# Block products for six of sixteen k-tile pairs in the second product of both MLPs of a two-layer decoder

## The chip, the cores and the metric

The kernel runs on one core of a Trainium2 chip. The metric is the device time of one execution in microseconds. The engines named below are PE (TensorE, matmuls; its weight loads are shown apart as PEld), DVE (VectorE), ACT (ScalarE), POOL (GpSimd) and SP (SyncE, which issues the DMAs here).

## What is computed

The reference is a decoder of two layers on 256 tokens with 1024 features, all in float32. Each layer is a mixer (attention on the tokens, differential in layer A and with one shared K/V in layer B, and attention to a fixed memory of 256 rows), and then an MLP of 1024 to 4096 to 1024:

```python
def _sq_relu_mlp(h, w_up, w_down):
    u = jax.nn.relu(h @ w_up)
    return (u * u) @ w_down

# in each layer, after the mixer has been added to x
x = x + _sq_relu_mlp(_rmsnorm(x, a_norm_mlp[i]), a_w_up[i], a_w_down[i])
```

The change concerns the product `(u * u) @ w_down`: 256 x 4096 times 4096 x 1024, once in layer A and once in layer B.

## The kernel before, in words

**Precision.** Each float32 operand is split into a high part, rounded to the fast matmul type (fp32r), and the rest (low). A product is made of three passes: high by high, low by high, high by low. For weights, ACT makes the high part of a chunk of 128 x 1024 (`wh`, a cast, L330), and DVE subtracts it from the chunk to get the low part (`wl`, L332); both stand in `chunk`. There are 192 chunks in the order of use, four buffers `w` for what the DMAs bring, and six each for `wh` and `wl`.

**Layouts.** The residual `xT` is held turned, features on the partitions (8 tiles of 128 x 256 tokens). `mlp_up` computes u turned as well, 32 tiles (k) of 128 hidden units by 256 tokens, each with its high and its low part (the tiles B, `us`). Its scaling, squaring and splitting on ACT and DVE are L779 to L793.

**Second product of layer A** (`mlp`, in `wide`, L805 and L809). The weights are the stationary operand. For each of 8 output tiles m there are 4 chunks of 8 k-tiles; a k-tile costs one matmul over 512 columns (high weights by both parts of u side by side) and one over 256 (low weights by high u). The result is already turned and is added to `xT` by `add_x`, tile by tile, so norms and statistics of layer B (`done`) start while later tiles are computed.

**Second product of layer B** (`mlp_last`, L861). The output is in natural layout, tokens on the partitions: the parts of u are stationary (128 tokens at a time, index hf), the weights move with 512 columns (index c). Four accumulators (hf, c) in PSUM, the banks `t`, take 32 k-tiles of three matmuls each. The last `HELD` = 6 k-tiles are kept back and done cell by cell, so that the final norm of one cell runs beside the products of the next. The residual has been turned to natural layout before by 16 transposes (L845).

**Order of the work.** The kernel is written as steps with an engine, an estimated time and keys for what they read and write. `Plan.order` then places them by list scheduling: among ready steps of an engine the lowest priority number goes first, and the number is the place in the program less a shift from the table `EARLY`, one for each kind of step and layer (`w` is the splitting of weights, `nat` the products of a mixer, `stat` the statistics, and so on). Buffers of a class are handed out in order. The engines then run their instructions in that fixed order and wait on semaphores. The stationary loads (PEld) run beside the matmuls.

Of the kernel before, what the change touches and what calls it, by code (L numbers as in the profile page):

```python
# [24 lines left out]
HELD = 6  # L25
CW = 1024
# [5 lines left out]
EARLY.update(wA=14, wB=40, memA=-47, memB=133, natA=84, natB=18, statA=-67, statB=98, ropeA=-143, ropeB=-86,  # L32
             scoreA=-56, scoreB=-10, ptA=23, ptB=73, pvB=-40, finA=160, finB=-72, evacA=46, evacB=53, prepA=151,
             prepB=46, normA=96, normB=44)
# [185 lines left out]
def t_mm(n, passes=1):  # L220
    return passes * (n / 2.4 + 13.5)
# [3 lines left out]
def tile_hybrid(ctx: ExitStack, tc: tile.TileContext, xa, xb, memt, xnat, mnat, w0, wall, consts, fgain, out):  # L225
    nc = tc.nc
# [20 lines left out]
    def bank(cls):  # L247
        return buf(cls, [128, 512], F32, psum)
# [4 lines left out]

    def fixed(shape, nm, dt=F32):
        return const.tile(shape, dt, name=name(nm))
# [18 lines left out]
    vb = fixed([128, 2, 12, 64], "vb")  # L274

# [356 lines left out]
    def plain_T(p, rs, causal):  # L632
# [4 lines left out]
        if par is None:  # L637
            pp = [Buf("ppa", lambda slot: ppx[:, slot]) for _ in range(2)]
        else:
            pp = [part(par, "ppb", 512) for _ in range(2)]  # L640
# [127 lines left out]
    def mlp_up(st):  # L768
# [4 lines left out]
        for b in range(16):  # L773
# [16 lines left out]
            P.add(("act", t_act(512), lambda u=u: nc.scalar.activation(u.t, u.t, AF.Square)), [u], [u])  # L790
            P.add(("act", t_act(512), lambda u=u, t=us[b // 2], k0=k0: nc.scalar.copy(t.t[:, k0:k0 + 2, 0], u.t)),
# [6 lines left out]
    def ukeys(us, k):  # L798
        return [(us[k // 4], k // 2), (us[k // 4], k // 2, 1)]
# [16 lines left out]

    def mlp(st, done):
        us = mlp_up(st)
        for m in range(8):
            ps = bank("acc")  # L820
            for c in range(4):
                wh, wl = chunk()
                wide(ps, wh, wl, lambda k, c=c: us[2 * c + k // 4].t[:, k % 4], lambda k, c=c: ukeys(us, 8 * c + k),
                     c == 0, c == 3)
            add_x(m, ps, 0)
            add_x(m, ps, S)
            done(m)
        st_["pieces"] = 2

    def mlp_last(st):  # L830
# [19 lines left out]
        us = mlp_up(st)  # L850
        pss = {cell: bank("t") for cell in cells}
        ch = []

        def mm(k, hf, c, c0=0, c1=512, ps=None, k0=0):
            wh, wl = ch[k]
            ps = ps or pss[hf, c]

            def emit():
                uh, ul = [us[k // 4].t[:, k % 4, i, hf * 128:(hf + 1) * 128] for i in range(2)]
                for i, (a, b) in enumerate(((uh, wh), (ul, wh), (uh, wl))):  # L860
                    nc.tensor.matmul(ps.t[:, c0:c1], a, b.t[:, c * 512 + c0:c * 512 + c1],  # L861
                                     start=(k == k0 and i == 0), stop=(k == 31 and i == 2), skip_group_check=True)
            P.add(("pe", t_mm(c1 - c0, 3), emit), ukeys(us, k) + [(wh, c), (wl, c)], [ps])
        held = 32 - HELD
        for k in range(32):
            ch.append(chunk())
            if k < held:
                for hf, c in cells:
                    mm(k, hf, c)
# [3 lines left out]
        for hf in range(2):  # L873
            ss, part_, r = fixed([128, 4], "ss"), fixed([128, 1], "part"), fixed([128, 1], "rstd")
            for c in range(2):
# [5 lines left out]
                for i in range(2):  # L881
                    if last:
                        for k in range(held, 32):
                            mm(k, hf, c, 256 * i, 256 * i + 256, tail if i else None, held if i else 0)
                        ps = tail if i else ps
# [271 lines left out]
def _layout(inp):  # L1157
# [18 lines left out]
    def down(w):  # L1176
        return w.reshape(4, 8, 128, 8, 128).transpose(3, 0, 2, 1, 4).reshape(32, 128, CW)
# [49 lines left out]
```

## Time and profile before

| | us |
|---|---|
| three runs | 605.34, 606.75 (median), 984.32 |
| the profiled execution | 606.42 |
| its span, first to last instruction | 604.6 |
| PE busy in the span | 592.3 (98%) |
| DVE busy | 438.6 (73%) |
| ACT busy | 377.2 (62%) |

The span is what the trace shows; the profiled execution's own time is 1.8 us longer. Shares of busy time are means over stages with different limits. A matmul's recorded duration holds its way through the array, and the next one begins before it ends, so what a row of matmuls costs is read from start to start. In the same way a DVE instruction may begin a little before the recorded end of the one ahead of it.

In time order the span holds: the mixer of layer A to about 127 us, the first product of its MLP to 216 us, the second to 305 us, the mixer of layer B to about 420 us, the first product of its MLP to 510 us, the second to 596 us, and the final norm and output.

### The profile page before, as it was taken

How to read it: one execution, taken by the hardware profiler on the slowest of the kernel's cores; microseconds unless marked ns; L12 is line 12 of the kernel's file. 1: busy time of each engine (PE TensorE's matmuls, PEld its weight loads, DVE VectorE, ACT ScalarE, POOL GpSimd, SP SyncE). 2: the span in 40 equal slices, each digit the busy share in tenths (PEclk: the TensorE clock that was granted, in tenths of full speed). 3: DMA queues.
4: the chain of work that ended last, by engine and by line, in shares of the span. 5: the costliest groups of instructions: out<-in, count | busy, mean ns of one | idle time of the engine just before them, and what ended most of it. 6: DMA issues, size and time to landing. Idle time of an engine off the chain costs nothing.

```text
span 604.6 us, 9476 instructions
## 1 busy us (share of the span) xinstructions
PE 592.3 (98%) x3430; PEld 505.1 (84%) x3430; DVE 438.6 (73%) x800; ACT 377.2 (62%) x771; POOL 55.6 (9%) x67
## 2 busy tenths in 40 slices
PE   8999999999999999999999999999999999999995
PEld 6778878988888888888888887889888888888884
DVE  6689997689887865656777788876888787544435
ACT  6878787576766654444665776776686666443422
POOL 0031020140000000101001123001300000000002
PEclk9989999999999999999999999999999999999998
DMA  8964733436655555555566435344565555555501
GB/s 317 335 206 149 261 108 107 156 129 206 217 201 181 201 178 197 185 186 194 180 208 237 145 105 171 109 140 147 185 226 178 197 184 194 189 185 198 191 20 69
DMA packets 29999, 108.39 MB, mean 179 GB/s; under 512 B 3328, under 2 KB 3328, under 8 KB 29696
## 3 DMA queue, kind: packets, MB, share of 16 engines
q1 hardware_dynamic: 29664, 107.26, 52.9%
q8 instruction: 27, 0.44, 0.3%
q10 hardware_dynamic: 288, 0.52, 0.2%
q14 instruction: 20, 0.16, 0.1%
HBM read 106.72 MB, written 1.05 MB: 178 GB/s over the span
## 4 chain that ended last, share of the span: by engine, by line
PE 93%; DMA 3%; DVE 2%; ACT 1%; issue 0%; SPq 0%; ACTq 0%
PE acc L805 29%; PE acc L493 19%; PE acc L809 15%; PE t L861 14%; PE acc L759 7%; DMA w<-wall 3%; PE t L580 2%; PE t L618 2%; PE t L675 1%; PE t L551 1%; DVE wl L332 1%; DVE xT L745 0%; ACT wh L330 0%; PE acc L861 0%; PE t L845 0%
## 5 line engine op out<-in xcount | busy, mean ns | idle before, releaser
L332 DVE TENSOR_TENSOR wl<-w,wh 128x512 fp32r<-128x512 f32 (+1 forms) x256 | 245.4, 979 | 116.7 <-ACT wh L330 114.3
L330 ACT CAST wh<-w 128x512 fp32r<-128x512 f32 (+1 forms) x256 | 208.8, 840 | 177.1 <-PE acc L805 90.6
L805 PE MATMUL acc<-xn,wh 128*128 128x512 f32 x512 | 131.3, 396 | 0.5 <-DVE xn L348 0.5
L805 PEld LDWEIGHTS acc<-xn,wh 128*128 128x128 f32 x512 | 91.1, 188 | 18.5 <-DVE xn L348 1.8
L493 PE MATMUL acc<-wh,xn 128*128 128x512 f32 x256 | 86.1, 401 | 0.9 <-ACT xn L346 0.9
L861 PE MATMUL t<-wh,B 128*128 128x512 f32 (+1 forms) x256 | 77.2, 384 | 0.0
L809 PEld LDWEIGHTS acc<-xn,wl 128*128 128x128 f32 x512 | 68.1, 188 | 5.6
L809 PE MATMUL acc<-xn,wl 128*128 128x256 f32 x512 | 69.1, 277 | 0.0
L805 PE MATMUL acc<-B,wh 128*128 128x512 f32 x256 | 64.1, 392 | 0.0
L493 PEld LDWEIGHTS acc<-wh,xn 128*128 128x128 f32 x256 | 48.0, 188 | 12.9 <-issue 1.5
L861 PEld LDWEIGHTS t<-wh,B 128*128 128x128 f32 x256 | 47.7, 188 | 9.5
L805 PEld LDWEIGHTS acc<-B,wh 128*128 128x128 f32 x256 | 46.0, 189 | 8.2
L493 PE MATMUL acc<-wl,xn 128*128 128x512 f32 x128 | 50.4, 394 | 0.1
L759 PE MATMUL acc<-B,wh 128*128 128x256 f32 x256 | 50.5, 289 | 0.0
L861 PE MATMUL t<-wl,B 128*128 128x512 f32 (+1 forms) x128 | 49.2, 384 | 0.0
L759 PEld LDWEIGHTS acc<-B,wh 128*128 128x128 f32 x256 | 41.0, 191 | 1.0 <-issue 0.8
L446 POOL TENSOR_TENSOR sqa<-sqa,sq 128x256 f32<-128x256 f32 x21 | 20.7, 988 | 226.5 <-ACT sq L445 225.9
L809 PEld LDWEIGHTS acc<-B,wl 128*128 128x128 f32 x256 | 34.9, 190 | 2.5
L759 PE MATMUL acc<-B,wl 128*128 128x256 f32 x128 | 36.1, 282 | 0.0
L527 POOL TENSOR_TENSOR ropet<-ropes,consts 128x256 f32<-128x256 f32 (+1 forms) x28 | 25.0, 912 | 120.4 <-ACT ropes L516 98.4
L809 PE MATMUL acc<-B,wl 128*128 128x256 f32 x256 | 35.7, 282 | 0.0
L599 ACT ACTIVATE B<-t,nm 128x128 f32<-128x128 f32 (+1 forms) x64 | 27.0, 441 | 7.6 <-DVE nm L595 5.7
(179 smaller groups left out, 727.1 us busy)
## 6 DMA issues: line engine op xcount, KB each, us to landing
w<-wall SPq DMA_DIRECT2D x191, 512.0 KB, 3.3
w<-memt SPq DMA_DIRECT2D x4, 512.0 KB, 4.8
B<-xnat SPq DMA_DIRECT2D x1, 1024.0 KB, 7.8
B<-mnat SPq DMA_DIRECT2D x1, 1024.0 KB, 8.3
xT<-xa SPq DMA_DIRECT2D x1, 540.0 KB, 3.6
w<-w SPq DMA_DIRECT2D x2, 256.0 KB, 3.6
xT<-xb SPq DMA_DIRECT2D x1, 512.0 KB, 6.3
consts<-consts SPq DMA_DIRECT2D x1, 256.5 KB, 4.4
```

Source lines behind the costliest of these rows:

```text
L330: P.add(("act", t_act(n), lambda sl=sl: nc.scalar.copy(h.t[:, sl], w.t[:, sl])), [(w, x) for x in q], [(h, x) for x in q])
L332: P.add(("dve", t_dve(n), lambda sl=sl: nc.vector.tensor_sub(l.t[:, sl], w.t[:, sl], h.t[:, sl].bitcast(F32))), [(w, x) for x in q] + [(h, ...
L446: P.add(("pool", t_pool(S), lambda: nc.gpsimd.tensor_tensor(self.acc.t, self.acc.t, sq.t, op=OP.add)), [sq, self.acc], [self.acc])
L493: nc.tensor.matmul(pss[hf].t[:, c0:c1], a(k)[:, ts], b.t[:, o + c0:o + c1], start=(k == 0 and i == 0), stop=(k == KT - 1 and i == 2))
L527: nc.gpsimd.tensor_tensor(t.t[:, 0:nh, e:e + 32], zs.t[:, 0:nh, 32 - e:64 - e], b(sin[:, e:e + 32]), op=OP.mult)
L580: nc.tensor.matmul(sp[hd].t[:, c], qk[a].t[r, qb * 128:(qb + 1) * 128], qk[b].t[r, S:S + c.stop - c.start], start=(qb == 0 and i == 0 and ...
L599: nc.scalar.activation(p[hd].t[:, c], sp[hd].t[:, c], AF.Exp, bias=nm[hd][:, qb:qb + 1], accum_out=ss[:, hd, qb:qb + 1])
L618: nc.tensor.transpose(ps.t[:, i * 128:(i + 1) * 128], p.t[:, j * 128:(j + 1) * 128], ident)
L759: nc.tensor.matmul(o, a.t[:, ws], x(k), start=(n == 0 and m % 2 == 0 and i == 0), stop=(n == KT - 1 and i == 2), skip_group_check=True)
L805: nc.tensor.matmul(ps.t, wh.t[:, k * 128:(k + 1) * 128], x(k).rearrange("p a s -> p (a s)"), start=start and k == 0, stop=stop and k == 7, ...
L809: nc.tensor.matmul(ps.t[:, 0:S], wl.t[:, k * 128:(k + 1) * 128], x(k)[:, 0], start=False, stop=stop and k == 7, skip_group_check=True)
L861: nc.tensor.matmul(ps.t[:, c0:c1], a, b.t[:, c * 512 + c0:c * 512 + c1], start=(k == k0 and i == 0), stop=(k == 31 and i == 2), skip_group ...
```

## The change

In both MLPs the second product treats the pairs of k-tiles 1, 3, 5, 7, 9 and 11 of 16 (`FAST`) as a product of two 2 x 2 matrices of blocks: 2 halves of the tokens by 2 k-tiles, times 2 k-tiles by 2 halves of the output columns. Instead of 8 block products it makes 7, of sums and differences of the blocks (Strassen's scheme, in Winograd's form). A block product is three matmuls of 512 columns, as before.

The four sums of blocks of u that this takes are made in the first product by four subtractions and additions of 128 x 128 on DVE (`block_sums`, in `mlp_up`); they are kept in buffers that are idle there (`ppx`, `vb`, `mv`), and are split into high and low in the second product, into tiles of `xn`. Four sums of weight blocks are made by DVE from the two loaded chunks (`diff`, four of 128 x 512, into the new buffer `wsum`), and then three chunks and a half are split for such a pair where two were. Four more accumulators, the banks `acc` (`more`), take the partial products, and `gather` adds them into the outputs after pair 11.

The second product of layer A takes the natural layout of layer B's (`natural_down`). Its last 8 k-tiles are done for output columns 0 to 511 first and then for 512 to 1023, with the weights laid out for that in `down`. Each half is added to the gathered part, turned back by transposes (8 for a half), and added to `xT`. The table `EARLY` has other numbers for all kinds of steps.

```diff
+FAST = (1, 3, 5, 7, 9, 11)
...
-EARLY.update(wA=14, wB=40, memA=-47, memB=133, natA=84, natB=18, statA=-67, statB=98, ropeA=-143, ropeB=-86,
+EARLY.update(wA=40, wB=-21, memA=20, memB=31, natA=25, natB=64, statA=-44, statB=-119, ropeA=-90, ropeB=9, scoreA=-92,
...
+            if b in sums:
+                dst, keys = sums[b]
+                def blocks(u=u, dst=dst):
+                    a = [u.t[:, k, hf * 128:hf * 128 + 128] for hf in range(2) for k in range(2)]
+                    s = [dst()[:, i * 128:i * 128 + 128] for i in range(4)]
+                    nc.vector.tensor_add(s[0], a[2], a[3])
+                    nc.vector.tensor_sub(s[1], s[0], a[0])
+                    nc.vector.tensor_sub(s[2], a[0], a[2])
+                    nc.vector.tensor_sub(s[3], a[1], s[1])
...
+        def fast_pair(n, j):
...
+            split(0, wb(0, 0), [wk[0]], 512)
+            diff(0, wb(0, 1), wb(0, 0), wk[:2])
+            split(1, lambda: w[1].t, wk[2:])
+            diff(1, wb(1, 1), lambda: t(0), [wk[3]] + rk(0))
+            split(2, lambda: t(0, 2), rk(0) + rk(1))
+            diff(2, wb(1, 1), wb(0, 1), [wk[1], wk[3]])
+            diff(3, wb(1, 0), lambda: t(1), [wk[2]] + rk(1))
+            split(3, lambda: t(2, 4), rk(2) + rk(3))
...
+            for ps, a, ak, x, c, last in (
+                    (more[0], u_(2 * j, 0), k0, 0, 0, end), (pss[0, 0], u_(2 * j + 1, 0), k1, 1, 0, False),
+                    (pss[0, 1], s_(3), ks, 1, 1, False), (more[1], s_(0), ks, 2, 0, end),
+                    (more[2], s_(1), ks, 2, 1, end), (more[3], s_(2), ks, 3, 0, end),
+                    (pss[1, 0], u_(2 * j + 1, 1), k1, 3, 1, False)):
+                product(ps, a, wcol(x, c), 0, 512, last, ak + [h[x], l[x]])
...
     def mlp(st, done):
-        us = mlp_up(st)
-        for m in range(8):
-            ps = bank("acc")
-            for c in range(4):
-                wh, wl = chunk()
-                wide(ps, wh, wl, lambda k, c=c: us[2 * c + k // 4].t[:, k % 4], lambda k, c=c: ukeys(us, 8 * c + k),
-                     c == 0, c == 3)
-            add_x(m, ps, 0)
-            add_x(m, ps, S)
-            done(m)
+        us = mlp_up(st, block_sums())
...
+        for c in range(2):
+            for k in range(part, 32):
...
+            for hf in range(2):
+                y, ps = ys[hf, c], pss[hf, c]
+                P.add(("dve", t_dve(512), lambda y=y, ps=ps: nc.vector.tensor_add(y.t, y.t, ps.t)), [y, ps], [y])
...
+                            nc.tensor.transpose(ps.t[:, i * S + hf * 128:i * S + hf * 128 + 128],
+                                                ys[hf, c].t[:, o:o + 128], ident)
```

Three places show how the order of instructions moves. On DVE, within the second product of layer A, the row before is that of two output tiles; `xT` and `xn` are the residual and the next layer's input:

```order
L332 TENSOR_TENSOR wl_2670<-w_2586,wh_2661 128x1024
L348 SCALAR_TENSOR_TENSOR xn_67<-xT_66,xn_67 128x256
L332 TENSOR_TENSOR wl_2695<-w_2608,wh_2687 128x1024
L332 TENSOR_TENSOR wl_2717<-w_2630,wh_2709 128x1024
L745 TENSOR_TENSOR xT_66<-xT_66,acc_2642 128x256
L332 TENSOR_TENSOR wl_2742<-w_2659,wh_2731 128x1024
```

Now one pair done as before and one fast pair fill this row (L338 is the old subtraction, L902 the sums of weight blocks, L895 the subtractions of the fast pair):

```order
L902 TENSOR_TENSOR wsum_78<-w_2916 128x512
L338 TENSOR_TENSOR wl_2947<-w_2875,wh_2941 128x1024
L902 TENSOR_TENSOR wsum_78<-w_2928,wsum_78 128x512
L902 TENSOR_TENSOR wsum_78<-w_2928,w_2916 128x512
L902 TENSOR_TENSOR wsum_78<-w_2928,wsum_78 128x512
L338 TENSOR_TENSOR wl_2973<-w_2904,wh_2961 128x1024
L895 TENSOR_TENSOR wl_2980<-w_2916,wh_2968 128x512
L895 TENSOR_TENSOR wl_2987<-w_2928,wh_2978 128x1024
L895 TENSOR_TENSOR wl_2999<-wsum_78,wh_2992 128x1024
L895 TENSOR_TENSOR wl_3011<-wsum_78,wh_3004 128x1024
```

The same ten rows stand there once for each of the later pairs of pairs; the earlier ones have a subtraction of 128 x 512 more, for the sums of u (L921).

On PE, at the end of the second product of layer A (L871, into the `t` banks), rows of the memory's keys and values for layer B (L499, into `acc`) now stand between the last products and the transposes that turn the second half (L990; `ql` holds the two cells of that half):

```order
L871 MATMUL t_2596<-wh_3128,B_518_2557 128x512 x2
L871 MATMUL t_2596<-wl_3135,B_518_2557 128x512
L499 MATMUL acc_3284<-wh_3250,wh_3148 128x512
L499 MATMUL acc_3284<-wl_3268,wh_3148 128x512
L499 MATMUL acc_3284<-wh_3250,wl_3154 128x512
L499 MATMUL acc_3296<-wh_3250,wh_3148 128x512
L499 MATMUL acc_3296<-wl_3268,wh_3148 128x512
L499 MATMUL acc_3296<-wh_3250,wl_3154 128x512
L499 MATMUL acc_3284<-wh_3261,wh_3148 128x512
L499 MATMUL acc_3284<-wl_3280,wh_3148 128x512
L499 MATMUL acc_3284<-wh_3261,wl_3154 128x512
L990 MATMUL t_3325<-ident_122,ql_3071 128x128
```

Before, the products of layer A ended and all 48 of the memory block followed, with no transpose among them.

On SP, the loads at the start of the kernel (`xnat` and `mnat` are the tokens and the memory in natural layout, for their statistics, `memt` the memory turned, `wall` the chunks of weights) stood in this order:

```order
L307 DMA consts_68<-consts 128x513
L307 DMA w_282<-wall 128x1024
L307 DMA w_298<-wall 128x1024
L307 DMA w_311<-wall 128x1024
L307 DMA B_133_325<-xnat 128x2048
L307 DMA w_354<-wall 128x1024
L307 DMA w_367<-memt 128x1024
L307 DMA w_376<-memt 128x1024
L307 DMA w_388<-wall 128x1024
L307 DMA B_147_401<-mnat 128x2048
```

With the new table they stand in this one:

```order
L313 DMA consts_68<-consts 128x513
L313 DMA B_126_283<-xnat 128x2048
L313 DMA w_310<-wall 128x1024
L313 DMA w_321<-wall 128x1024
L313 DMA w_333<-wall 128x1024
L313 DMA w_345<-wall 128x1024
L313 DMA B_138_353<-mnat 128x2048
L313 DMA w_382<-memt 128x1024
L313 DMA w_406<-memt 128x1024
L313 DMA w_417<-wall 128x1024
```

The tokens in natural layout have moved ahead of three chunks of weights, and the memory in natural layout ahead of the turned memory and of the first chunk that the memory block uses.

## Rows read from the trace of the kernel before

**Rows 1.** The page's head and busy time of two engines over the span.

```profile
span 604.6 us, 9476 instructions
...
PE 592.3 (98%) x3430; PEld 505.1 (84%) x3430; DVE 438.6 (73%) x800; ACT 377.2 (62%) x771; POOL 55.6 (9%) x67
```

**Rows 2.** PE in time around layer A's second product: start, duration, instructions.

```profile
215.66 1.99 PE L805 MATMUL acc<-B,wh 128*128 128x512 f32 x8
217.49 1.12 PE L809 MATMUL acc<-B,wl 128*128 128x256 f32 x8
...
304.08 1.12 PE L809 MATMUL acc<-B,wl 128*128 128x256 f32 x8
305.03 0.40 PE L493 MATMUL acc<-wh,wh 128*128 128x512 f32 x1
```

**Rows 3.** The chain that ended last, layer B's second product: start, length.

```profile
510.47 85.13 PE t L861 x384
```

**Rows 4.** PE in time there: start, duration; three matmuls from 511.01 to 511.69.

```profile
511.01 0.61 PE L861 MATMUL t<-wh,B 128*128 128x512 f32 x2
511.46 0.39 PE L861 MATMUL t<-wl,B 128*128 128x512 f32 x1
511.69 0.61 PE L861 MATMUL t<-wh,B 128*128 128x512 f32 x2
```

**Rows 5.** PE in time, eight of the 16 transposes ahead of layer B's MLP.

```profile
419.25 1.03 PE L845 MATMUL t<-ident,xT 128*128 128x128 f32 x8
420.04 0.71 PE L805 MATMUL acc<-xn,wh 128*128 128x512 f32 x2
```

**Rows 6.** Stretches: us; busy (count) of PE, PEld, DVE, ACT, POOL; clock; DMA.

```profile
0.00:20.00 20.00, 17.88 (x94) 14.31 (x95) 13.70 (x32) 12.89 (x25) 0.44 (x5) 1.00 0.88 327
...
127.00:216.00 89.00, 88.50 (x515) 76.99 (x514) 75.09 (x114) 61.63 (x104) 5.48 (x6) 1.00 0.58 190
216.00:306.00 90.00, 90.00 (x517) 79.15 (x516) 55.94 (x74) 44.41 (x66) 5.97 (x6) 1.00 0.57 190
```

**Rows 7.** DVE in time, first product of layer A: start, duration.

```profile
149.30 1.23 DVE L332 TENSOR_TENSOR wl<-w,wh 128x1024 fp32r<-128x1024 f32 x1
150.44 0.41 DVE L781 TENSOR_TENSOR u<-u,acc 128x256 f32<-128x256 f32 x1
150.77 1.22 DVE L332 TENSOR_TENSOR wl<-w,wh 128x1024 fp32r<-128x1024 f32 x1
151.91 0.68 DVE L793 TENSOR_TENSOR B<-u,B 128x512 fp32r<-128x512 f32 x1
152.51 0.68 DVE L787 SCALAR_TENSOR_TENSOR u<-u,rb 128x512 f32<-128x512 f32 x1
153.11 0.41 DVE L781 TENSOR_TENSOR u<-u,acc 128x256 f32<-128x256 f32 x1
```

**Rows 8.** Groups of the span: busy, mean ns; idle before, and its releaser.

```profile
L332 DVE TENSOR_TENSOR wl<-w,wh 128x1024 fp32r<-128x1024 f32 x128 | 157.5, 1230 | 97.5 <-ACT wh L330 97.5
L330 ACT CAST wh<-w 128x1024 fp32r<-128x1024 f32 x128 | 134.7, 1052 | 148.1 <-PE acc L805 89.7 <-PE t L861 40.6 <-PE acc L759 16.6
```

**Rows 9.** PE in time near the start: first uses of the memory block's weights.

```profile
28.04 0.40 PE L493 MATMUL acc<-wh,xn 128*128 128x512 f32 x1
29.01 0.50 PE L493 MATMUL acc<-wh,wh 128*128 128x512 f32 x1 [0.57 <-ACT ropes L516]
31.74 0.79 PE L493 MATMUL acc<-wl,wh 128*128 128x512 f32 x1 [2.23 <-DVE wl L332]
...
34.03 0.63 PE L493 MATMUL acc<-wh,wh 128*128 128x512 f32 x1
34.46 0.48 PE L493 MATMUL acc<-wl,wh 128*128 128x512 f32 x1
```

**Rows 10.** The chain that ended last, near the start: two loads of weights.

```profile
9.54 5.62 DMA w<-wall
...
20.33 6.72 DMA w<-wall
```

More of the change, by code (lines that the diff above doesn't have):

```diff
@@ L31 @@
 EARLY = {k + l: 0 for k in KINDS for l in "AB"}
[L32 to L34 removed]
+EARLY.update(wA=40, wB=-21, memA=20, memB=31, natA=25, natB=64, statA=-44, statB=-119, ropeA=-90, ropeB=9, scoreA=-92,
+             scoreB=-56, ptA=128, ptB=-59, pvA=-41, pvB=145, finA=153, finB=85, evacA=38, evacB=167, prepA=148,
+             prepB=38, normA=120, normB=40)
 LOOK = 100
@@ L252, in part, with ppx_buf @@
         return Buf(cls, lambda slot: parent.t[:, slot, 0:width], parent)
+    def ppx_buf():
+        return Buf("ppa", lambda slot: ppx[:, slot])
     def fixed(shape, nm, dt=F32):
@@ L274, in tile_hybrid @@
     vb = fixed([128, 2, 12, 64], "vb")
+    wsum = fixed([128, 2048], "wsum")
     ones_b = fixed([128, 128], "ones_b", BF)
@@ L637, in plain_T @@
         if par is None:
-            pp = [Buf("ppa", lambda slot: ppx[:, slot]) for _ in range(2)]
+            pp = [ppx_buf() for _ in range(2)]
         else:
@@ L766, in out_proj, with mlp_up @@
                 done(m)
-    def mlp_up(st):
+    def mlp_up(st, sums=()):
         st.rstd()
@@ L790, in mlp_up @@
             P.add(("act", t_act(512), lambda u=u: nc.scalar.activation(u.t, u.t, AF.Square)), [u], [u])
+            if b in sums:
[7 more added lines that the diff above has]
+                    nc.vector.tensor_sub(s[3], a[1], s[1])
+                P.add(("dve", 4 * t_dve(128) + 100, blocks), [u], keys, port=True)
             P.add(("act", t_act(512), lambda u=u, t=us[b // 2], k0=k0: nc.scalar.copy(t.t[:, k0:k0 + 2, 0], u.t)),
@@ L815, in wide, with block_sums @@
                   [x for j in range(k, k + 4) for x in keys(j)] + [(wl, k // 4)], [ps])
-    def mlp(st, done):
-        us = mlp_up(st)
-        for m in range(8):
-            ps = bank("acc")
-            for c in range(4):
-                wh, wl = chunk()
-                wide(ps, wh, wl, lambda k, c=c: us[2 * c + k // 4].t[:, k % 4], lambda k, c=c: ukeys(us, 8 * c + k),
-                     c == 0, c == 3)
-            add_x(m, ps, 0)
-            add_x(m, ps, S)
-            done(m)
+    def block_sums():
+        sums = {}
+        for i, j in enumerate(FAST):
+            if i < 2:
+                b = ppx_buf()
+                dst, keys = (lambda b=b: b.t), [b]
+            elif i < 5:
+                dst = lambda i=i: vb.rearrange("p a b e -> p (a b e)")[:, (i - 2) * 512:(i - 1) * 512]
+                keys = [("vb", n, hf) for n in range(2) for hf in range(2)]
+            else:
+                dst, keys = (lambda: mv.rearrange("p a b e -> p (a b e)")), [("mv", 0), ("mv", 1)]
+            sums[j] = dst, keys + [("s", j)]
+        st_["sums"] = sums
+        return sums
@@ L849, in mlp_last, with gather, add, to @@
             xs[hf, c] = x
-        us = mlp_up(st)
+        us = mlp_up(st, block_sums())
         pss = {cell: bank("t") for cell in cells}
[L852 to L863, printed above, removed]
-        held = 32 - HELD
[L865 to L869, printed above, removed]
+        def gather(more):
+            v = buf("u", [128, 2, S])
+            vt = lambda: v.t.rearrange("p a s -> p (a s)")
+            def add(dst, a, b, r, w, port=False):
+                P.add(("dve", t_dve(512), lambda: nc.vector.tensor_add(dst(), a(), b())), r, w, port=port)
+            def to(cell, src, key, port=False):
+                x = xs[cell]
+                add(lambda: x.t, lambda: x.t, src, [(x, 0), (x, 1), key], [(x, 0), (x, 1)], port)
+            r1, r5, r6, r7 = more
+            P.add(("act", t_act(512, True), lambda: nc.scalar.copy(vt(), r1.t)), [r1], [v])
+            to((0, 0), lambda: r1.t, r1)
+            add(vt, vt, lambda: r6.t, [v, r6], [v])
+            to((0, 1), vt, v, True)
+            to((0, 1), lambda: r5.t, r5)
+            to((1, 1), lambda: r5.t, r5)
+            add(vt, vt, lambda: r7.t, [v, r7], [v])
+            to((1, 0), vt, v, True)
+            to((1, 1), vt, v, True)
+        held = 32 - HELD
+        mm = natural_down(us, pss, 32, held, gather, wsum, lambda a: [("wsum", a)], 4)[0]
         x, ps, tail = xs[1, 1], pss[1, 1], bank("acc")
@@ L883, in mlp_last @@
                         for k in range(held, 32):
-                            mm(k, hf, c, 256 * i, 256 * i + 256, tail if i else None, held if i else 0)
+                            mm(k, hf, c, 256 * i, 256 * i + 256, tail if i else None)
                         ps = tail if i else ps
@@ L1176, in down @@
     def down(w):
-        return w.reshape(4, 8, 128, 8, 128).transpose(3, 0, 2, 1, 4).reshape(32, 128, CW)
+        w = w.reshape(32, 128, CW)
+        return np.concatenate([w[:24], w[24:].reshape(4, 2, 128, 2, 512).transpose(3, 0, 2, 1, 4).reshape(8, 128, CW)])
     def mix(q, k, v, qm, mem, second):
```

96 lines of the change are left out of this document (added).

## The prediction

> **What bounds the kernel now.** I read the page first: the span is 604.6 us, PE is busy for 98% of it and DVE for 73% [rows 1]. Busy PE may still be slow PE, so next came PE in time, from start to start. In layer A's second product eight wide and eight narrow matmuls follow one another without a gap from 215.66 to 305.03 us, and the mixer's products begin at once behind them [rows 2]: 89.4 us for 32 chunks, 2.79 us each. In layer B's second product three matmuls of 512 columns start every 0.68 us, 0.2267 us each [rows 4], and the chain that ended last runs through 384 of them in one piece of 85.1 us [rows 3]. So in both stages nothing but the number of columns sets the time. The only idle time of PE that a change of order can touch lies near the start: 0.57 and 2.23 us at 28 to 32 us [rows 9], where a load of weights ended the wait [rows 10]. The forecast is therefore a count of matmuls, if DVE, which gets most of the new work, keeps up.
>
> **Layer A's products.** In natural layout 32 k-tiles cost 4 cells by 3 matmuls each, 384. A fast pair makes 7 x 3 = 21 where two k-tiles made 24, so six save 18, and 366 are left. At 0.2267 us that is 83.0 us, against 89.4: minus 6.4 us. Of this 4.1 are the block products; 2.3 are the layout, whose 384 would take 87.1 us, because the wide form's 2.79 us for a chunk is more than 12 x 0.2267 = 2.72. The new transposes, 16 in all, are like those ahead of layer B's MLP, where eight take 0.79 us from start to start [rows 5]: plus 1.6 us. Three changes of matmul kind around them I put at 0.1 us each, an estimate from the 0.1 us of a transpose: plus 0.3. Layer A: minus 4.5 us.
>
> The Trainium skill, "TensorE: Matmul & The Clock Gate", Part 4, gives about 275 ns for a transpose in a kernel. By that the 16 cost 4.4 us and layer A gains 1.7. The trace does not agree: the starts are 0.1 us apart [rows 5], and they decide.
>
> **Layer B's products.** The same 18 matmuls of 512 columns go: minus 4.1 us. The last six k-tiles, held back for the norm, and the end behind them stay as they are.
>
> **DVE in the second products.** From start to start a subtraction of 128 x 1024 takes 1.14 us, one of 128 x 512 0.60 and one of 256 columns 0.33 [rows 7]. The ten rows of the order for a normal and a fast pair are five of each of the first two sizes: 5 x 1.14 + 5 x 0.60 = 8.7 us; the split of the sums of u makes it 9.3 in the earlier ones. PE needs 24 + 21 = 45 matmuls, 10.2 us. So DVE fits with 0.9 us to spare in 10, where it was busy for 56 of 90 us before [rows 6]. ACT's casts, two and three and a half chunks at 1.05 us [rows 8] and the half-size one for u, are 6.3 of 10.2. Buffers: a fast pair takes four of the six `wh` and `wl`, and its products free them in order, after 0.7, 2.0, 3.4 and 4.8 us. The next fast pair's last subtraction can follow the last release by a cast of 1.05 and its own 1.14 us, some 7.2 us into a period of 10.2. Cost: 0, with PE's own products as the cover. If the cover is gone, PE waits once for each of the 12 fast pairs, and the later products queue behind the waiting matmul, with the `acc` and `t` banks held. Bounds: below, 0, as DVE removes no PE work; above, the rival's 35 us.
>
> **DVE in the first products.** 24 small operations are added in each MLP. At no more than 0.33 us, the row of 256 columns, they are 8 us or less; the first fast pair's 7 us are also made there. The stage had DVE busy for 75 of 89 us [rows 6], so by recorded durations it is now full at 90; as a start comes some 0.09 us before the recorded end ahead of it [rows 7] and there were 114 instructions, nearer 80 by starts. The first fast pair is due only 5.4 us after the stage's end, behind a normal pair. Cost 0, at most 2 us in each layer if DVE is late there.
>
> **The end of layer A's second product.** Before, residual tiles were finished throughout; now four wait for the end. Between the last product and the first transpose of that half the order has three steps of three memory products, 9 x 0.2267 = 2.0 us, in which DVE adds two cells (2 x 0.60, with one weight subtraction of 0.60 between). 45 of the 48 memory products stand before the last transposes and the 48 products of layer B's keys, the first to read the new tiles, follow: the last tiles are read more than 8 us later. An addition of 0.33, a cast and a subtraction per tile fit. Cost 0; with no cover at all the chain is two additions of cells (1.2 us), eight transposes (0.8), four additions to tiles (1.3) and eight subtractions for two norms (8 x 0.33 = 2.7), 6.0 us.
>
> **The new table.** The mixers' products are the same instructions in another sequence. PE is idle for 12.3 us of the whole span [rows 1], so there is little to win; I take 0, from minus 1 to plus 3 us. At the start, `xnat` now stands ahead of three chunks. The loads run at 327 GB/s there [rows 6], so this 1.05 MB delays the chunk that landed at 15.2 us [rows 10] by 3.2 us, and PE would begin its second block some 2.5 us late. `mnat` likewise goes ahead of the chunk that landed at 27.05; it would land near 30.2, and cast and subtraction make it ready near 31.6, where PE waited until 31.74 before [rows 9]. So a wait is moved rather than added: 0, from minus 4.2 (the rival below) to plus 4.
>
> **Sum.** Minus 4.5, minus 4.1 and zeros make minus 8.6 us. Against the profiled execution, 606.42 us (its span of 604.6 and 1.8 outside), that is 597.8; the median of the three runs, 606.75, is 0.3 above it. I predict 598.
>
> **Rivals.** *PE waits in every fast pair* (slower). DVE waited 97.5 us for ACT's casts over 128 subtractions, 0.76 each [rows 8]. If each of the five casts in a pair of pairs costs DVE that wait, it needs 9.3 + 3.8 = 13.1 us for PE's 10.2, and 12 fast pairs lose 2.9 each: 598 + 35 = 633. It decides for slower by over 2% (above 618.9) from 1.7 us a pair. For it: cast and subtraction alternate through few buffers. Against: those casts were waiting for PE to free buffers, 148 us in all [rows 8]; the waits were slack. *DVE has no slack.* If every subtraction costs its recorded 1.23 or 0.68 us, a period is 10.2 us of DVE against 10.2 of PE, and any hitch is lost: some 0.25 us for each of 12 pairs, 601. The rows speak against it: the next one starts 0.09 us before the recorded end [rows 7]. The Trainium skill, "VectorE: DVE Perf Modes", section "The DRAIN you can't avoid", says that the next operation does not start until the pipeline is empty, which is this rival; the trace does not agree. *The start heals.* If the new order of loads removes the waits of 0.57 and 2.23 us, and with them the slow stretch behind, where six matmuls took 2.72 us and not 1.36 [rows 9], 4.2 us go: 594. Against it is the sum of bytes, which is the same. *The turned end shows*: 6 us at the end of layer A, 604.
>
> **How the numbers follow.** The forecast has a chance of 0.62, with its own range of 595 to 602; DVE without slack 0.11, the turned end 0.09, the healed start 0.11, PE waiting in every fast pair 0.07. Two per cent, about what a measurement of this kernel can tell from no change, is 12 us here: below 594.6 only part of the healed start and a low forecast lie, 0.08 in all; above 618.9 only the waits in fast pairs at their worse, 0.05. The rest, 0.87, is within. The range, 593 to 605, takes in the small rivals and leaves out the slow one.
>
> **What would show it.** Right: layer A's second product near 85 us with its transposes, the chain's piece in layer B 4.1 us shorter than 85.1, matmuls 0.2267 us apart throughout, DVE busy for over 90% in the first two thirds of each, and PE idle only near the start. Wrong: idle PE put down to the subtractions of the fast pairs or to the sums, over 0.2 us each; a gap before the transposes or before the first products of layer B; more than 3 us of idle PE before 40 us. The prediction falls if the matmuls in the fast pairs start further apart than 0.23 us.

## The result, and the profile after

The changed kernel takes 599.36 us (median of 4 runs, 598.01 to 600.37), the kernel before 606.75 (median of 3 on the same chip, 605.34 to 607.21; a fourth, disturbed run of 984.32 counts in no comparison). The ratio is 0.988, 95% interval 0.985 to 0.991: 7.4 us less. The forecast was 598, with a range of 593 to 605.

The page of after, its head and engines (answers to [rows 1]):

```profile
span 596.2 us, 9398 instructions
...
PE 586.0 (98%) x3282; PEld 494.6 (83%) x3282; DVE 506.8 (85%) x937; ACT 405.5 (68%) x812; POOL 55.8 (9%) x67
```

PE has 148 instructions and 6.3 us less, DVE 137 instructions and 68 us more. PE is still busy for 98%, so the new work of DVE lies beside it. PE in time, layer A's second product, its transposes and what follows (start, duration; answers to [rows 2, 5]):

```profile
214.74 0.63 PE L871 MATMUL t<-wh,B 128*128 128x512 f32 x2
...
288.36 1.04 PE L990 MATMUL t<-ident,qh 128*128 128x128 f32 x8
289.15 0.70 PE L871 MATMUL t<-wh,B 128*128 128x512 f32 x2
...
300.16 0.39 PE L499 MATMUL acc<-wh,wh 128*128 128x512 f32 x1
...
302.20 0.60 PE L990 MATMUL t<-ident,ql 128*128 128x128 f32 x4
...
309.47 0.60 PE L990 MATMUL t<-ident,ql 128*128 128x128 f32 x4
```

From 214.74 to 300.16 are 85.42 us. In them lie six products of the memory block (L499), 1.36 us, and the first eight transposes, 0.79; the MLP's own products are 83.3 us, where before they were 89.4. The other transposes, four at a time, take 0.35 us twice to the next start, so all 16 are 1.5 us. None of these rows has an idle time in brackets. Layer B's second product, first row and last row (answers to [rows 3, 4]):

```profile
505.81 0.63 PE L871 MATMUL t<-wh,B 128*128 128x512 f32 x2
...
589.05 0.28 PE L871 MATMUL acc<-wl,B 128*128 128x256 f32 x1
```

These are 83.24 us. The same two rows of before start at 510.31 and 597.48, 87.17: 3.9 us less. The start (answers to [rows 9]):

```profile
6.40 1.06 PE L499 MATMUL acc<-wh,xn 128*128 128x512 f32 x2
7.25 0.63 PE L499 MATMUL acc<-wl,xn 128*128 128x512 f32 x1
...
29.47 0.40 PE L499 MATMUL acc<-wh,xn 128*128 128x512 f32 x1
30.10 0.50 PE L499 MATMUL acc<-wh,wh 128*128 128x512 f32 x1 [0.23 <-ACT wh L336]
30.83 0.50 PE L499 MATMUL acc<-wl,wh 128*128 128x512 f32 x1 [0.23 <-DVE wl L338]
31.16 0.39 PE L499 MATMUL acc<-wh,wl 128*128 128x512 f32 x1
31.39 0.40 PE L499 MATMUL acc<-wh,wh 128*128 128x512 f32 x1
```

The waits of 0.57 and 2.23 us have shrunk to 0.23 each, and the matmuls 0.43 us apart behind the second are gone: here they start 0.23 apart. Yet layer A's second product begins only 0.9 us earlier than before (214.74, 215.66). A part was lost ahead of the waits: PE's last matmul before them, the 130th in both traces, starts at 29.47 where before it was 28.04, since in this trace eight matmuls between 5.4 and 9 us start 0.43 us apart or more (6.40 to 7.25 is two of them; the granted clock is recorded as 1.00 there). Stretches: the first 20 us, layer A's first product, the first two thirds of its second (answers to [rows 6]):

```profile
0.00:20.00 20.00, 18.20 (x88) 14.94 (x89) 12.04 (x30) 13.48 (x29) 0.44 (x5) 1.00 0.91 325
126.00:214.90 88.90, 88.41 (x515) 76.99 (x514) 81.88 (x143) 61.52 (x103) 5.54 (x6) 1.00 0.57 190
214.90:275.60 60.70, 60.70 (x268) 50.16 (x268) 54.10 (x65) 38.83 (x46) 0.00 (x0) 1.00 0.54 187
```

DVE is the third engine in each row: 92% of the first product and 89% of the fast pairs' stretch, where PE is busy for all 60.70. DVE in time, one whole period of a fast and a plain pair:

```profile
243.67 1.82 DVE L895 TENSOR_TENSOR wl<-w,wh 128x512 fp32r<-128x512 f32 x2
...
249.65 0.69 DVE L902 TENSOR_TENSOR wsum<-w 128x512 f32<-128x512 f32 x1 [1.88 <-DMA w<-wall]
...
254.33 1.82 DVE L895 TENSOR_TENSOR wl<-w,wh 128x512 fp32r<-128x512 f32 x2
```

10.66 us pass, 1.88 of them in wait for a load: 8.8 us of work, for PE's period of 10.2 (DVE's next period is 9.95 us). So the span's 8.4 us come from the start (0.9), layer A's second product with its turn (89.4 against 83.3 + 1.5, 4.6) and layer B's (3.9), less 1.0 us between the two.

### The profile page after: what moved, and what is told of

It is laid out like the page before. It is cut to its first block, busy times and chain, and to the rows that moved or that the text cites. A ratio compares the mean times of both kernels' runs of the same rounds, so it can differ in the third digit from the quotient of the medians.

```text
span 596.2 us, 9398 instructions
## 1 busy us (share of the span) xinstructions
PE 586.0 (98%) x3282; PEld 494.6 (83%) x3282; DVE 506.8 (85%) x937; ACT 405.5 (68%) x812; POOL 55.8 (9%) x67
## 4 chain that ended last, share of the span: by engine, by line
PE 87%; DMA 4%; DVE 4%; ACT 4%; issue 1%; SPq 0%; ACTq 0%
PE t L871 22%; PE acc L823 20%; PE acc L499 15%; PE acc L827 10%; PE acc L765 7%; PE acc L871 6%; PE t L586 2%; PE t L624 2%; PE t L681 1%; DVE wl L338 1%; DMA B<-xnat 1%; DMA w<-wall 1%; ACT wh L336 1%; DMA w<-memt 1%; PE t L557 1%
## 5 line engine op out<-in xcount | busy, mean ns | idle before, releaser
L336 ACT CAST wh<-w 128x512 fp32r<-128x512 f32 (+1 forms) x232 | 182.8, 818 | 115.8 <-PE acc L823 42.6
L338 DVE TENSOR_TENSOR wl<-w,wh 128x512 fp32r<-128x512 f32 (+1 forms) x232 | 213.6, 942 | 37.2 <-ACT wh L336 36.7
L871 PE MATMUL t<-wh,B 128*128 128x512 f32 (+1 forms) x368 | 111.9, 386 | 0.0
L499 PE MATMUL acc<-wh,xn 128*128 128x512 f32 x256 | 86.7, 405 | 0.5 <-ACT xn L352 0.5
L871 PEld LDWEIGHTS t<-wh,B 128*128 128x128 f32 x368 | 68.6, 188 | 13.8
L871 PE MATMUL t<-wl,B 128*128 128x512 f32 (+1 forms) x184 | 71.0, 386 | 0.0
L499 PEld LDWEIGHTS acc<-wh,xn 128*128 128x128 f32 x256 | 49.0, 191 | 12.9 <-issue 1.4
L499 PE MATMUL acc<-wl,xn 128*128 128x512 f32 x128 | 51.1, 399 | 0.2 <-DVE wl L338 0.2
L765 PEld LDWEIGHTS acc<-B,wh 128*128 128x128 f32 x256 | 41.2, 191 | 0.9 <-issue 0.7
L871 PEld LDWEIGHTS t<-wl,B 128*128 128x128 f32 x184 | 34.6, 188 | 7.0
L765 PE MATMUL acc<-B,wl 128*128 128x256 f32 x128 | 36.2, 282 | 0.0
L894 ACT CAST wh<-wsum 128x1024 fp32r<-128x1024 f32 x24 | 25.3, 1054 | 9.1 <-PE acc L823 3.7
L895 DVE TENSOR_TENSOR wl<-wsum,wh 128x1024 fp32r<-128x1024 f32 x24 | 28.9, 1222 | 1.9 <-ACT wh L894 1.4
L499 PEld LDWEIGHTS acc<-wl,xn 128*128 128x128 f32 x128 | 24.6, 192 | 5.1 <-DVE wl L338 0.5
```

What stands on the lines that cost most here:

```text
L336: P.add(("act", t_act(n), lambda sl=sl: nc.scalar.copy(h.t[:, sl], w.t[:, sl])), [(w, x) for x in q], [(h, x) for x in q])
L338: P.add(("dve", t_dve(n), lambda sl=sl: nc.vector.tensor_sub(l.t[:, sl], w.t[:, sl], h.t[:, sl].bitcast(F32))), [(w, x) for x in q] + [(h, ...
L499: nc.tensor.matmul(pss[hf].t[:, c0:c1], a(k)[:, ts], b.t[:, o + c0:o + c1], start=(k == 0 and i == 0), stop=(k == KT - 1 and i == 2))
L765: nc.tensor.matmul(o, a.t[:, ws], x(k), start=(n == 0 and m % 2 == 0 and i == 0), stop=(n == KT - 1 and i == 2), skip_group_check=True)
L871: nc.tensor.matmul(ps.t[:, c0:c1], x, y, start=start and i == 0, stop=stop and i == 2, skip_group_check=True)
L894: P.add(("act", t_act(m), lambda: nc.scalar.copy(h[x].t[:, :m], src())), keys, [h[x]])
```

## Experiments

Each is an edit of the kernel after, timed against the kernel before.

**Which part of the change earns it: no block products.**

```diff
-FAST = (1, 3, 5, 7, 9, 11)
+FAST = ()
...
-                P.add(("dve", t_dve(512), lambda y=y, ps=ps: nc.vector.tensor_add(y.t, y.t, ps.t)), [y, ps], [y])
+                P.add(("dve", t_dve(512), lambda y=y, ps=ps: nc.vector.tensor_copy(y.t, ps.t)), [ps], [y])
```

> The kernel after without block products: all 16 pairs of k-tiles in plain products, layer A still in natural layout and turned. Theory (columns alone set the time): 36 matmuls of 512 columns come back at 0.2267 us, so 599.4 + 8.2 = 607.5 us; layer A's products take 87.1 us and layer B's 87.3. Rival (part of the gain is the table's, at the start or between the layers, and the block products bring less): 603 to 605.

606.82 us, ratio to before 0.9996 (0.9978 to 1.0013). PE in time, first row of layer A's second product, first row behind it, and first and last row of layer B's:

```profile
214.78 0.63 PE L871 MATMUL t<-wh,B 128*128 128x512 f32 x2
...
304.12 0.39 PE L499 MATMUL acc<-wh,wh 128*128 128x512 f32 x1
...
509.83 0.63 PE L871 MATMUL t<-wh,B 128*128 128x512 f32 x2
...
597.00 0.28 PE L871 MATMUL acc<-wl,B 128*128 128x256 f32 x1
```

89.34 and 87.17 us, against 85.42 and 83.24: 3.9 us in each layer are the block products, 7.5 by the medians. All the rest of the change (layout, transposes, table) makes no difference beyond the interval, 1.3 us: the natural products, 89.34 less the same 2.15 of other work, are 87.2 us against 89.4, the start is 0.9 earlier (214.78), and the transposes (1.5) and 1.1 us between the layers use most of that up. The theory's 607.5 was right; the rival, that the table earns a part, falls.

**The table.**

```diff
-EARLY.update(wA=40, wB=-21, memA=20, ...
+EARLY.update(wA=14, wB=40, memA=-47, ...
```

> The kernel after with the table of due times of the kernel before. Theory (the table moves waits and removes almost none): within 1 us of 599.4; layer A's second product would start near 215.7 us as before, 0.8 later, and the mixers of layer B would win that back. Rival (the start heals by the table, and this is worth several us): 602 to 604. Rival (the new table costs something between the layers): 597.

599.94 us, ratio 0.987 (0.984 to 0.989): no difference from after. The places differ, and not as expected. PE in time, the first row behind layer A's second product, the second half's transposes, the first row of layer B's second product:

```profile
301.51 0.39 PE L499 MATMUL acc<-wh,wh 128*128 128x512 f32 x1
...
302.87 1.04 PE L990 MATMUL t<-ident,ql 128*128 128x128 f32 x8
...
507.69 0.63 PE L871 MATMUL t<-wh,B 128*128 128x512 f32 x2
```

These are 206.2 us, 205.4 without the eight transposes, and 205.3 before (305.03 to 510.31). With the new table they are 206.3 (205.65, less 0.7 for transposes, and 1.36 for the six products done earlier): so the 1.0 us lost between the layers is the new table's, where the second rival had it, though its 597 did not come. The old table loses at the start instead: layer A's first product began at 126.78 and its second at 217.45, 2.7 us behind after. How much of that is the table's can't be told, for the first product begins at different times in runs whose early code is the same, as with the kernel after and the one with four transposes for each (below):

```profile
124.05 1.26 PE L823 MATMUL acc<-xn,wh 128*128 128x512 f32 x4
```

```profile
127.67 1.25 PE L823 MATMUL acc<-xn,wh 128*128 128x512 f32 x4
```

The second of these had its first 20 us at this rate, 302 GB/s against 325:

```profile
0.00:20.00 20.00, 17.54 (x83) 14.11 (x83) 10.88 (x28) 12.65 (x27) 0.44 (x5) 1.00 0.86 302
```

So the start scatters by 3.6 us. It goes with the rate of the loads: among nine traces with the new table and the same buffers, the six with 320 to 333 GB/s in the first 20 us reach this place at 123.9 to 124.9, the three with 302 to 314 at 126.6 to 127.7. That the rate is the cause isn't shown, and it isn't all: with the old table it is 124.99 in before and 126.78 here, at 327 and 326 GB/s. No table's gain of less than this scatter can be read from one trace.

**The price of a transpose.**

```diff
-                    for i in range(2):
+                    for i in [0, 1] * 4:
```

> The kernel after with each of the 16 transposes of layer A done four times, 48 more on PE. Theory (a transpose costs its 0.1 us from start to start, as in the rows): 599.4 + 4.8 = 604.2. Rival (about 275 ns for each, the Trainium skill's figure in TensorE: Matmul & The Clock Gate, Part 4; no term of the sum): 599.4 + 13.2 = 612.6.

604.57 us, ratio 0.995 (0.993 to 0.997): 5.2 us for 48 more. PE in time there:

```profile
292.00 3.66 PE L990 MATMUL t<-ident,qh 128*128 128x128 f32 x32
295.41 0.70 PE L871 MATMUL t<-wh,B 128*128 128x512 f32 x2
```

32 in 3.41 us, 0.107 each. The row of before was right: in the groups of after a transpose lasts 272 to 279 ns, but in a sequence it costs the 0.1 us to the next start.

**DVE's cover: the same difference of weights done two, three and five times in each fast pair** (shown for five; the other two have 1 and 2 in place of the 4).

```diff
-                P.add(("dve", t_dve(512), lambda: nc.vector.tensor_sub(t(a), x(), y())), keys, rk(a), port=True)
+                def emit():
+                    for _ in range(1 + 4 * (a == 2)):
+                        nc.vector.tensor_sub(t(a), x(), y())
+                P.add(("dve", t_dve(512), emit), keys, rk(a), port=True)
```

> The kernel after with one subtraction of 128x512 done twice in each fast pair (the result stays the same): 0.60 us more of DVE in each period of 45 matmuls, 10.2 us. Theory (DVE has 0.9 to 1.1 us to spare in a period): 599 to 600, PE without idle time in the fast pairs. Rival (DVE has no slack): 12 x 0.60 = 7.2 us more, 606.6.

> The kernel after with the difference of weights done three times in each fast pair: 1.2 us more, between the one more that cost nothing (599.4) and the four more that cost 25 us. Theory of the sum alone (9.3 + 1.2 = 10.5 us of DVE in a period of 10.2): 0.3 for each of 12 pairs, 602 to 604. Theory with the wait for the load on top (0.7 to 1.1 us in each period that cannot be used): 11.2 to 11.6 us against 10.2, 1.0 to 1.4 for some 11 pairs, 609 to 615.

> The kernel after with the same subtraction of 128x512 done five times in each fast pair: 2.4 us more of DVE in each period. Theory (0.9 to 1.1 us to spare, the rest falls on PE): 1.3 to 1.5 us lost in each of some 10 to 12 periods, 612 to 618, with idle time of PE in the fast pairs put down to DVE. Rival (no slack at all): 12 x 2.4 = 28.8, 628. Rival (DVE runs far ahead through the buffers and the plain chunks at the end make it good): 599 to 602.

599.43 us (ratio 0.986, 0.984 to 0.989) with one more; 608.96 (1.002, 0.999 to 1.005) with two; 624.8 (1.029, 1.027 to 1.030) with four. By these times one is free, as the theory said. Two more come out between the two theories, at the lower edge of the second, and don't decide between them; four more lie above the theory's 612 to 618 and below the 628 of no slack. In the same stretch of layer A, after and with one more:

```profile
222.40:273.60 51.20, 51.20 (x227) 42.29 (x226) 44.81 (x51) 30.34 (x33) 0.00 (x0) 1.00 0.60 209
```

```profile
222.40:273.60 51.20, 51.20 (x227) 42.30 (x226) 47.49 (x56) 30.25 (x33) 0.00 (x0) 1.00 0.57 203
```

DVE's busy time grows by 2.7 us, PE's stays full. In layer B, though, PE waits once in this run, so the cover is at its edge there: the second product takes 84.2 us against 83.2. PE's wait (us in total, times, longest):

```profile
PE t L871 <- DVE wl L338: 0.6, 1, 0.6
```

With four more, PE waits eleven times for L338, the subtraction of a plain pair's chunk, which stands behind the fast pair's work in DVE's queue. PE's largest wait (us in total, times, longest), one stretch, and PE and DVE in time:

```profile
PE t L871 <- DVE wl L338: 15.3, 11, 2.8
```

```profile
255.20:258.80 3.60, 3.60 (x9) 2.88 (x10) 3.60 (x4) 0.89 (x1) 0.00 (x0) 0.53 0.71 259
```

```profile
255.18 0.79 PE L871 MATMUL t<-wl,B 128*128 128x512 f32 x1 [2.79 <-DVE wl L338]
255.77 1.05 PE L871 MATMUL t<-wh,B 128*128 128x512 f32 x2
256.62 0.63 PE L871 MATMUL t<-wl,B 128*128 128x512 f32 x1
```

```profile
260.36 0.69 DVE L904 TENSOR_TENSOR wsum<-w 128x512 f32<-128x512 f32 x1 [1.23 <-DMA w<-wall]
...
262.71 3.59 DVE L904 TENSOR_TENSOR wsum<-w,w 128x512 f32<-128x512 f32 x5
266.22 0.68 DVE L904 TENSOR_TENSOR wsum<-w,wsum 128x512 f32<-128x512 f32 x1
...
273.13 0.69 DVE L904 TENSOR_TENSOR wsum<-w 128x512 f32<-128x512 f32 x1 [1.09 <-DMA w<-wall]
```

Two sizes in my expectations were wrong. The five take 3.51 us from start to start, not 3.0: each repetition writes the tile that the one ahead wrote, and such a one starts some 0.725 us later, not 0.60 (four of 0.725 and one of 0.61). So four more are 2.9 us, two 1.45 and one 0.72. And behind the wait of 2.79 us matmuls start 0.43 us apart at a granted clock of 0.53, the lower level; 13 such starts after the mixer of layer A are 13 x 0.2 = 2.6 us. They stand behind the two longest waits, 2.79 and 2.83 us, and none behind the next, 2.25 and 2.15. The period was 12.77 us (260.36 to 273.13): 11.7 of work and 1.1 of wait for a load. Not all of the 25 us lie in the second products: the first ones take 92.5 and 93.6 us against 90.7 and 91.8, 3.6 us in both together. The first fast pair's five differences are done there (at 206.30 us in layer A), and PE waits for L788, which empties an `acc` bank behind them.

**Is it the wait for the load?** Two runs tried that. One puts four more operations where no loaded block is held, in the split of the sums of u:

```diff
-            P.add(("dve", t_dve(512), lambda: nc.vector.tensor_sub(sl, src(), sh.bitcast(F32))), sk + kh, kl, port=True)
+            def emit():
+                for _ in range(5):
+                    nc.vector.tensor_sub(sl, src(), sh.bitcast(F32))
+            P.add(("dve", t_dve(512), emit), sk + kh, kl, port=True)
```

> The kernel after with four more operations of 128x512 in each fast pair, as in the run that repeated the difference of weights four more times (624.8 us), but now the split of the sums of u is the one repeated: the same 2.4 us of DVE, at a place where no loaded block of weights waits to be given back. Theory (in that run each period had 11.7 us of DVE work and on top 1.1 us in which DVE waited for a load, because the repeated operation reads a weight block and holds its buffer 2.4 us longer): the wait goes, a period is 11.7 us against 10.2, 1.5 for each of some 11 periods, 614 to 618, with few waits of DVE for loads. Rival (the place does not matter, DVE's waits come with its work): 623 to 626.

> The split of the sums of u done five times in each fast pair, a second look for its trace. Theory (the wait for the load comes from the subtraction of the pair's second block and is there whatever else DVE does): waits of DVE for loads as in the kernel with the repeated difference, 1 us in each period. Rival (other work in the place of the wait covers it, and the loss of 27 us lies in the first products, where the first sums are split ahead of time): no waits for loads, first products 3 us or more longer than 90.6 and 91.7.

626.88 us, ratio 1.033 (1.030 to 1.036): not the 614 to 618 of the theory, and 0.9 above the rival's 623 to 626, for which the place does not matter. In the trace of the second run (625.46 us) DVE's waits for loads are 5.1 us in four, against 7.9 in seven; both first products are as long as in after (90.7 and 91.8 us), so the rival's place is wrong as well: all the loss lies in the second products, 98.7 and 96.9 us against 85.4 and 83.2. The other pair, both with the difference of weights done five times, has five buffers for weight blocks, and a control with four:

```diff
-caps = {"w": 4, ... "u": 2, "sq": 2, "sqa": 2, ... "o": 4,
+caps = {"w": 5, ... "u": 1, "sq": 1, "sqa": 1, ... "o": 2,
```

> The kernel after with the difference of weights done five times in each fast pair (624.8 us before), and five buffers for loaded weight blocks instead of four; to make room one buffer each fewer of u, of the squares' and two of the mixer's outputs, so only the second products, first to last matmul, are read. Theory (the wait of 1.1 us in each period is for a load that can start only when the subtraction of the pair's second block has freed its buffer; a fifth buffer takes it off): 1.5 us lost in each of five periods, 92 to 93 us in layer A and 90 to 91.5 in layer B. Rival (the loss is DVE's work and its order alone): 95 in both, as with four.

> The same with the same buffers of u, squares and outputs, and four for weight blocks: the control of the run with five. Both theories: second products of 95 us in both layers, with DVE's wait of about 1 us for a load in each period.

First product row and the first row behind the last in layer A, with five buffers and with four:

```profile
226.77 0.63 PE L871 MATMUL t<-wh,B 128*128 128x512 f32 x2
...
323.62 0.39 PE L499 MATMUL acc<-wh,wh 128*128 128x512 f32 x1
```

```profile
226.25 0.63 PE L871 MATMUL t<-wh,B 128*128 128x512 f32 x2
...
323.11 0.39 PE L499 MATMUL acc<-wh,wh 128*128 128x512 f32 x1
```

96.85 and 96.86 us; in layer B 94.4 and 94.9. The fifth buffer gained nothing, where 92 to 93 and 90 to 91.5 were expected. But this pair, one run each, does not settle why. In the second products DVE's waits for loads are 1.4 us with five buffers and only 3.2 with four, not 1 us in each period, so there was little to take off. And PE's waits there are 2.3 us shorter with five (12.4 against 14.7), while 34 matmuls start 0.43 us apart against 21, some 2.6 us more: the two cancel. What both tries show is that the loss does not follow DVE's waits for loads. (The times of these two, 641.99 and 641.25 us, hold first products of 101.6 and 101.8 us in layer A, with one buffer of u, and are not compared with the others.)

**Fast pairs side by side.**

```diff
-FAST = (1, 3, 5, 7, 9, 11)
+FAST = (1, 2, 3, 4, 5, 6)
```

> The kernel after with the six fast pairs next to one another (pairs 1 to 6), the same count of everything. Theory (a fast pair needs 7.0 us of DVE, 0.60 + 3 x 1.14 + 5 x 0.60, and 4.8 us of PE; only the plain pair between two of them, 2.3 against 5.4, pays for it): 2.2 us lost for each of the five that follow another, in each layer, 22 in all, less what one period of lead saves: 615 to 622. Rival (the buffers hold enough lead, or DVE is not what limits): 599 to 602.

610.88 us, ratio 1.006 (1.004 to 1.008): 11.5 us above after, below the range expected. DVE in time, one fast pair to the next, and the stretch of the six:

```profile
240.33 0.68 DVE L895 TENSOR_TENSOR wl<-w,wh 128x512 fp32r<-128x512 f32 x1
...
247.35 0.68 DVE L895 TENSOR_TENSOR wl<-w,wh 128x512 fp32r<-128x512 f32 x1
```

```profile
220.00:255.00 35.00, 31.29 (x131) 23.73 (x130) 35.00 (x44) 21.48 (x26) 0.00 (x0) 1.00 0.42 150
```

7.02 us for a pair, as worked out, and DVE busy for 35.00 of 35. The direction and DVE's price were right; the five pairs lost 5.5 to 7 us in a layer and not 11, so by that sum DVE entered them 4 to 6 us ahead, which no row shows. With the same counts of everything, the plain pair between two fast ones is worth more than the whole gain of the block products.

**The sums of u done four times.**

```diff
-                    nc.vector.tensor_add(s[0], a[2], a[3])
...
+                    for _ in range(4):
+                        nc.vector.tensor_add(s[0], a[2], a[3])
...
+                        nc.vector.tensor_sub(s[3], a[1], s[1])
```

> The kernel after with the four small operations for the sums of u done four times in each fast pair's block of the first product (same result): 72 more of 128x128 in each layer, 0.2 us each from start to start, 14.4 us. DVE was idle for 7.0 of 88.9 us there. Theory (DVE fills that first product to its edge, the spare 7 us are all there is): some 7 us lost in each layer, 610 to 616. Rival (spare time cannot be used, all of it is lost): 14.4 x 2, 628. Rival (DVE is well behind the path and runs ahead again): 599 to 601.

623.4 us, ratio 1.026 (1.024 to 1.029): 24 us lost, all in the first products (102.6 and 103.7 us against 90.7 and 91.8). DVE in time, one set of four; PE's waits; PE in time:

```profile
184.67 0.28 DVE L805 TENSOR_TENSOR vb<-u 128x128 f32<-128x128 f32 x1
184.99 0.29 DVE L806 TENSOR_TENSOR vb<-vb,u 128x128 f32<-128x128 f32 x1
185.20 0.29 DVE L807 TENSOR_TENSOR vb<-u 128x128 f32<-128x128 f32 x1
...
185.60 0.28 DVE L805 TENSOR_TENSOR vb<-u 128x128 f32<-128x128 f32 x1
```

```profile
PE acc L824 <- DVE u L788: 14.4, 11, 2.5
```

```profile
189.79 2.13 PE L824 MATMUL acc<-xn,wh 128*128 128x512 f32 x8 [1.00 <-DVE u L788]
```

A set is 0.93 us, not 0.8: the second operation reads what the first wrote and starts 0.32 later, the others 0.2. So 12 x 3 x 0.93 = 33.5 us were added and 24 lost. PE waits for L788, which empties its `acc` bank and stands in DVE's queue behind the small operations. The theory's place was right, its size too small (610 to 616): 16.7 us a layer were added and not 14.4, and 4.9 of the spare 7.0 were used. That the rest could not be used because it is spread over the whole stage is likely, but not shown.

The runs that load DVE, side by side. "At the lower clock" is the count of matmuls of 512 columns that start 0.43 us apart after 120 us, times 0.2:

| run | DVE added, us | lost against after, us | of it at the lower clock | absorbed for each of 12 pairs |
|---|---|---|---|---|
| one more | 12 x 0.72 = 8.7 | 0.1 | 0 | 0.7 |
| two more | 12 x 1.45 = 17.4 | 9.6 | 0 | 0.7 |
| four more | 12 x 2.9 = 34.8 | 25.4 | 2.6 | 1.0 |
| four behind | 34.8 | 27.5 | 5.0 | 1.0 |
| sums four times | 33.5 | 24.0 | 2.2 | 1.0 |

The times are medians from several sessions, in which the median of before itself lay between 606.75 and 607.76, so a loss holds to about 1 us. With one more all was absorbed but for layer B's 1.0 us. About 0.7 to 1.0 us for each fast pair costs nothing, and beyond that each us of DVE is a us of PE, wherever it stood in these runs.

## Why the prediction was right

- *Block products, minus 4.1 in each layer.* 3.9 in each. 18 matmuls fewer, and the pitch of 0.227 us held.
- *Layout, minus 2.3.* 87.2 against 89.4 us: minus 2.2.
- *Transposes, plus 1.6, and 0.3 for changes of kind.* 1.5 us in the trace, and 0.107 each in the run with four times as many. Behind each of the three groups the first matmul takes some 0.09 us more than 0.227 to the next start, 0.3 in all.
- *DVE in the second products, 0, with 0.9 us to spare in 10.* PE waits in no fast pair. The spare time is 0.7 to 1.0 us by the table, close to the 0.9 of the earlier periods; of the 1.5 that the sum left in the later ones (8.7 of 10.2) the table shows no sign. The rival in which PE waits in every fast pair is what the run with four more shows; it needed 2.9 us more of DVE. The rival of no slack falls with the run of one more: 8.7 us added, at most 1 lost.
- *DVE in the first products, 0 to 2.* 0: layer A's, from its first narrow matmul to the second product, takes 83.70 us in both kernels (131.96 to 215.66, now 131.04 to 214.74). But DVE is at 92% there (81.9 us busy, near the 80 forecast), with 7.0 us left, and the sums run shows that they are soon used up.
- *The end of layer A's second product, 0 of up to 6.* No gap stands ahead of the transposes, and 45 products of the memory block cover the additions, as counted.
- *The table, 0, from minus 1 to plus 3 in the mixers and minus 4.2 to plus 4 at the start.* The zero came out, the way to it did not. The prediction read the 2.23 us as a wait that a load ended, and let the later load move it; in before's chain that load landed at 27.05 us and PE went on at 31.74, with casts, `ropes` and DVE's queue between. The waits did not move but shrank (to 0.23 us each, with no matmul at half pace behind them): the rival's healed start, in the profiled execution. It was worth 0.9 us at 214.74 and not 4.2, and the table lost 1.0 us between the layers. That these two cancel is luck, the more as the start scatters. Old and new table give the same time.
- *Signs.* DVE was to be busy for over 90% in the first two thirds of a second product; it was 89% in layer A and 90% in layer B. The other signs came as named: no idle PE in fast pairs, no gap at the turn, no pitch above 0.23.

The sum was minus 8.6 us. The profiled executions differ by 8.4, the medians by 7.4. So close a match of the first is in part chance, as the start alone moves a single execution by up to 3.6 us; the terms that were measured apart (3.9 twice, 2.2, 1.5) carry the account.

What stays open: why DVE still waits for loads (seven waits of 0.7 us on average in after, seven of 1.1 with four more) and what a fifth buffer would bring without the longer stretches at the lower clock, and how much of the 3.6 us of scatter at the start a better order of loads could remove. None of these was tried further.

## What to carry to other kernels

Where one engine is busy all the time and its instructions run at their pitch, count its instructions: 18 matmuls of 512 columns fewer were worth 3.9 us a layer, and a change of layout (2.2 us) was worth little more than its transposes cost (1.8 with the changes of kind). Then give each new operation on the covering engine its price from start to start, period by period, and keep the slack in view: here one more operation in each fast pair was free, two cost about what the block products had brought (the run's ratio to before is 1.002, 0.999 to 1.005), and the same fast pairs without a plain pair between them cost more than that. A cover is best measured by adding to it until it breaks.

## What was not expected of the hardware

- DVE's pitch depends on what the operation ahead wrote. Independent operations of 128x512 start 0.60 us apart, ones that write the same tile again 0.725, which is 0.03 more than the recorded 0.69; of 128x128, independent ones start 0.20 apart and one that reads what the one ahead wrote 0.32. In the trace each of these later ones waits for a semaphore that the one ahead raises, so the overlap is missing where such a wait stands. The rule of the Trainium skill that the prediction weighed ("VectorE: DVE Perf Modes", "The DRAIN you can't avoid": the next operation waits for an empty pipeline) fits the dependent ones in these rows, not the independent ones; the same section adds that an operation that isn't held back starts earlier, and the independent ones agree with that.
- Behind a wait of 2.79 us PE's granted clock was 0.53 for 3.6 us, with matmuls 0.43 us apart and not 0.227. So some long waits are paid for a second time behind them: 2.6 of the 25.4 us there, 5.0 of the 27.5 with four behind. Which ones is not settled: in the run with four behind, such starts follow a wait of 2.56 us and none follow one of 3.57.
- The same early instructions brought PE to layer A's first product at 124.05 and at 127.67 us, with loads at 325 and 302 GB/s.
